# Retention values in one 512-wide pass with four resident weight slots, and sample state updates with zero-padded full-row operands

## The chip, the cores and the metric

The kernel runs on one core of a Trainium2 chip. The time is device microseconds (us) from the launch's first to its last instruction on that core, and runs are compared by their median. Five engines work in parallel, each through its own instruction queue in order: TensorE (PE, matmuls; PEld is its weight load), VectorE (DVE), ScalarE (ACT), GpSimd (POOL) and SyncE (SP, which here only issues DMAs). SBUF is the on-chip memory, PSUM the memory that matmuls write to.

## What is computed

One inference step of a two-layer decoder trunk for a prompt of 1024 tokens and a sample group of 8 sequences with 8 tokens each: layer 0 is sliding-window attention, layer 1 is retention in chunks of 128 tokens. The change touches layer 1 alone. Cut to it, the reference is:

```python
def retention_chunk(state, q, k, v, lg):          # one head: d = 256, e = 512
    a = jnp.einsum('bqhd,bshd->bhqs', q, k) * dmask[None]
    inner = jnp.einsum('bhqs,bshe->bqhe', a, v)
    cross = jnp.einsum('bqhd,bhde->bqhe', q, state) * decay
    new_state = jnp.exp(L * lg) * state + jnp.einsum('bshd,bshe->bhde', k_dec, v)
    return new_state, inner + cross

z = h @ w_in                  # (tokens, 1024) @ (1024, 6144): q 1024, k 1024, v 2048, gate 2048
q, k, v, g = jnp.split(z, [1024, 2048, 4096], axis=-1)
# prompt: 8 chunks of 128 tokens, state carried along; sample: one chunk of 8 tokens a sequence
y = (group_norm(o) * silu(g)) @ w_out
```

## The kernel before

All 1088 tokens (1024 of the prompt, 64 of the sample) go through each projection together. Each operand x of a projection is split into hi (rounded) and lo = x - hi, and a product is three matmuls: hi*hi, hi*lo, lo*hi. `split` does this with one ACT cast and one DVE subtraction (L281, L282).

**Weights.** They stream through in slots of 128x1024 numbers. `prep` takes the oldest raw slot (`wraw`, two buffers), splits it into `whi` and `wlo` (three buffers in `wpool`) and has SP load the next raw one; `slot` hands a ready pair to a projection. A pool named in `self.extra` for a slot number may hold that slot's split in place of `wpool`.

**Two forms of projection.** `pair_t` (and `quad_t`) keeps a weight slot stationary and streams 384 or 320 tokens (L135 to L137); it serves q, k, the gate and the output projections. `group_n` keeps 128 tokens stationary and streams weights, so that its result has tokens in rows; it serves the attention values (`first=True`) and, in layer 1, the retention values, 256 features at a time: two passes a head, each of two slots. A pass makes, for 8 token chunks and 8 slices of the inner dimension, three matmuls of 128x256 (L194 to L196), and for the sample chunk, whose stationary holds hi and lo side by side, two (L199, L200). Results go to the PSUM tile `pj` (two buffers, each of two halves of 512 columns), ACT scales them into `v1` (L871), POOL stores them to the DRAM scratch `s_v1` (L872).

**Layer 1.** `ret_qkv` for head 0 runs first. Then `weave` mixes, at `RATE_RET`, the projections of the rest (the gate of head h, then q, k, v of head h+1) with `ret_units`, a generator of 32 units, one for each head and chunk. A unit loads q, k and v back (`ret_load`), forms the masked scores (L944) and the transposed keys (L956), splits v (`split_v`), and in `ret_mid` makes the inner and cross products (L985 to L990) and the state update (L1002 to L1004), all of 128x512. The inner product of the first chunk is the first PE instruction of layer 1 that waits for v.

**Samples.** Beside the eight units of a head run eight steps of `ret_sample_step`. At the even ones the queries of four sequences, in `qpad`, multiply their stored states `s0`, each with 32 columns of the array (L1069, float32). At every step two sequences get their new state's increment: keys `ks` and values `vs` hold four sequences in 32 rows each (hi and lo twice), and one matmul takes the 32 rows of one sequence, `ks[r]` by `vs[r]` (L1080, PSUM tile `pa`, four buffers). DVE adds it to the scaled old state in place (L1083), POOL stores the new state (L1084). `ret_sample_load` has SP load four states for each even step (L1050, eight buffers) and, every fourth step, `ks` and `vs` (L1056, L1057).

**What sets the order.** The program text gives an order, but the tile framework's scheduler moves each instruction on each engine's queue by its own estimate of when its inputs are there. It puts single sample matmuls and pieces of a unit between the matmuls of a projection. Once built, each engine's order is fixed.

## Time and profile before

| | |
|---|---|
| median of 3 runs (lowest, highest) | 1697.99 us (1696.72, 1701.69) |
| the profiled execution | 1695.23 us |
| its span, first to last instruction | 1693.5 us, mean granted clock 0.999 |
| PE busy | 1668.0 us, 98% of the span |
| DVE, ACT, POOL busy | 988.7 (58%), 612.7 (36%), 340.0 (20%) us |
| DMA engines, mean traffic | 161 GB/s over the span |

A matmul's row gives its start and its latency; matmuls overlap, so what one costs the engine is the distance from its start to the next one's start, not its latency. Layer 1 up to the last unit lies between 655 and 1480 us of the span.

### The profile page before, as it was taken

To read this page: it belongs to the slowest core of one execution; us is meant where nothing else is said; L and a number is where in the kernel's file an instruction comes from. 1 tells how busy PE (TensorE), PEld (TensorE's weight loads), DVE (VectorE), ACT (ScalarE), POOL (GpSimd) and SP (SyncE) were. 2 spreads that over 40 slices of the span, in tenths; PEclk is the share of its full clock that TensorE was granted. 3 is DMA by queue.
4 is the path that set the end of the run, shared out by engine and by line. 5 is a ranking of instruction groups with operands and counts; after the bars stand their busy time and mean duration, and the time that the engine had idled before them with its cause. 6 is when DMAs were issued, how large, how long until landed. Compare 5 with 4: busy or idle time off the path is not lost.

```text
span 1693.5 us, 28264 instructions
## 1 busy us (share of the span) xinstructions
PE 1668.0 (98%) x10600; PEld 1583.5 (94%) x10600; DVE 988.7 (58%) x2184; ACT 612.7 (36%) x1365; POOL 340.0 (20%) x533
## 2 busy tenths in 40 slices
PE   8999999999999999999999999999999999999998
PEld 7989999988999999899999999999899988999998
DVE  7558787966248574246744655455744756443852
ACT  6245555777334341222222312322222432241421
POOL 1413312132001121211123212231122222200000
PEclk9999999999999999999999999999999999999999
DMA  8655646684315443254445544465454865482342
GB/s 288 174 142 154 168 118 170 178 273 166 119 36 173 144 146 119 80 165 154 155 165 183 184 154 160 151 188 177 146 163 146 279 199 172 167 256 86 122 143 87
DMA packets 178697, 273.15 MB, mean 161 GB/s; under 512 B 29968, under 2 KB 128336, under 8 KB 178528
## 3 DMA queue, kind: packets, MB, share of 16 engines
q1 hardware_dynamic: 141152, 177.94, 35.1%
q0 software_dynamic: 37408, 93.40, 15.7%
q8 instruction: 83, 1.36, 0.3%
q14 instruction: 54, 0.44, 0.1%
HBM read 173.45 MB, written 99.68 MB: 161 GB/s over the span
## 4 chain that ended last, share of the span: by engine, by line
PE 73%; issue 1%; DMA 0%; POOL 0%; ACT 0%; DVE 0%; POOLq 0%; ACTq 0%
PE pj L135 17%; PE pj L137 17%; PE pj L136 17%; PE pj L194 3%; PE pj L195 3%; PE pj L196 3%; PE pa L1080 1%; PE pa L1069 1%; PE pa L913 1%; PE pa L1002 1%; PE pa L1003 1%; PE pa L1004 1%; PE pa L944 1%; PE pa L987 1%; PE pa L986 1%
## 5 line engine op out<-in xcount | busy, mean ns | idle before, releaser
L135 PE MATMUL pj<-act,whi 128*128 128x384 f32 (+1 forms) x2160 | 711.9, 330 | 2.3 <-ACT ys L729 1.2
L137 PE MATMUL pj<-act,wlo 128*128 128x384 f32 (+1 forms) x2160 | 707.8, 328 | 0.0
L136 PE MATMUL pj<-act,whi 128*128 128x384 f32 (+1 forms) x2160 | 707.1, 327 | 0.0
L135 PEld LDWEIGHTS pj<-act,whi 128*128 128x128 f32 x2160 | 405.8, 188 | 11.7 <-issue 6.3
L137 PEld LDWEIGHTS pj<-act,wlo 128*128 128x128 f32 x2160 | 405.6, 188 | 4.2 <-issue 3.2
L136 PEld LDWEIGHTS pj<-act,whi 128*128 128x128 f32 x2160 | 405.8, 188 | 3.6 <-issue 2.0
L281 ACT CAST whi<-wraw 128x512 fp32r<-128x512 f32 (+1 forms) x226 | 127.9, 613 | 191.5 <-PE pj L136 150.6
L282 DVE TENSOR_TENSOR wlo<-wraw,whi 128x512 fp32r<-128x512 f32 (+1 forms) x226 | 146.7, 681 | 70.7 <-ACT whi L281 70.3
L194 PE MATMUL pj<-whi,act 128*128 128x256 f32 x528 | 149.0, 286 | 1.1 <-ACT v L871 0.6
L195 PE MATMUL pj<-wlo,act 128*128 128x256 f32 x528 | 148.7, 283 | 0.0
L196 PE MATMUL pj<-whi,act 128*128 128x256 f32 x528 | 147.9, 283 | 0.0
L194 PEld LDWEIGHTS pj<-whi,act 128*128 128x128 f32 x528 | 100.1, 191 | 7.2 <-issue 3.2
L195 PEld LDWEIGHTS pj<-wlo,act 128*128 128x128 f32 x528 | 101.0, 191 | 0.8 <-issue 0.2
L196 PEld LDWEIGHTS pj<-whi,act 128*128 128x128 f32 x528 | 100.6, 191 | 0.3 <-issue 0.2
L518 ACT ACTIVATE s_sb<-s_sb,nm 128x257 f32<-128x257 f32 (+2 forms) x136 | 65.7, 488 | 33.2 <-DVE nm L515 32.6
L871 ACT ACTIVATE v<-pj,rcol 128x256 f32<-128x256 f32 x64 | 29.9, 474 | 127.7 <-PE pj L196 91.7
L330 DVE TENSOR_TENSOR rp_a<-pj,cs 128x768 f32<-128x768 f32 (+1 forms) x39 | 35.6, 912 | 63.5 <-PE pj L137 63.5
L872 POOL DMA_DIRECT2D s_v<-v x64 | 35.4, 554 | 167.8 <-ACT v L871 167.6
L340 DVE TENSOR_TENSOR rp_b<-pj,rbc 128x768 f32<-128x768 f32 (+1 forms) x36 | 32.8, 910 | 50.8 <-PE pj L137 50.7
L959 ACT ACTIVATE kh<-pa,rdec 128x256 fp32r<-128x256 f32 (+1 forms) x36 | 17.0, 473 | 114.0 <-PE pa L956 113.4
L1083 DVE SCALAR_TENSOR_TENSOR s<-s,pa 128x512 f32<-128x512 f32 x64 | 42.2, 684 | 24.5 <-PE pa L1080 24.0
L342 ACT ACTIVATE rp_a<-rp_b 128x768 f32<-128x768 f32 (+1 forms) x36 | 29.2, 810 | 73.1 <-DVE rp_b L340 73.1
(233 smaller groups left out, 2556.6 us busy)
## 6 DMA issues: line engine op xcount, KB each, us to landing
wraw<-wt SPq DMA_DIRECT2D x110, 512.0 KB, 4.4
s<-st SPq DMA_DIRECT2D x64, 256.0 KB, 3.1
srs<-s POOLq DMA_DIRECT2D x64, 256.0 KB, 2.7
act<-s_og SPq DMA_DIRECT2D x48, 192.0 KB, 3.8
qst<-s_q SPq DMA_DIRECT2D x32, 256.0 KB, 4.5
qk<-s_qk SPq DMA_DIRECT2D x32, 256.0 KB, 3.5
s_v<-v POOLq DMA_DIRECT2D x64, 128.0 KB, 2.5
vv<-s_v SPq DMA_DIRECT2D x32, 256.0 KB, 2.7
```

The source lines that it names most:

```text
L135: mm(ps, hi[:, sl], a[c][:, 0], start=start and i == 0, stop=False)
L136: mm(ps, hi[:, sl], a[c][:, 1], start=False, stop=False)
L137: mm(ps, lo[:, sl], a[c][:, 0], start=False, stop=stop and i == last)
L194: mm(o, hi, w[0][:, sl], start=start, stop=False)
L195: mm(o, hi, w[1][:, sl], start=False, stop=False)
L196: mm(o, lo, w[0][:, sl], start=False, stop=stop)
L281: self.nc.scalar.copy(hi, x)
L282: self.nc.vector.tensor_tensor(out=lo, in0=x, in1=hi.bitcast(F32), op=ALU.subtract)
L330: nc.vector.tensor_tensor(out=ta, in0=ps, in1=self.cs[:, 0:1, c0:c0 + n].broadcast_to([P, 2, n]), op=ALU.mult)
L518: nc.scalar.activation(s[:, h, :], s[:, h, :], AF.Exp, bias=nm[:, h, :], scale=0.125, accum_out=den[:, h:h + 1])
L872: nc.gpsimd.dma_start(self.s_v1[h, i, :, g * 256:g * 256 + 256], st)
L1083: nc.vector.scalar_tensor_tensor(out=s0, in0=s0, scalar=float(gam ** 8), in1=pds[j], op0=ALU.mult, op1=ALU.add)
```

## The change

The retention values get their own routine, `group_v`: 512 features at a time in one pass a head, with four slots taken at once, so that one matmul streams 512 columns; a slot now holds two slices of 512 columns in place of four of 256. `group_n` keeps the attention values alone. The four splits are made earlier: `pair_t` for the keys calls `prep` also after the first half of its first two token blocks (`more`), and of the four slots of v the middle two are held in layer 1's own pool (`self.extra`); `wpool` keeps its three buffers. Results are evicted at 512 columns into the tile `rp_a`, and `v1` goes away.

In the sample update `kpad` holds, for each of four sequences, a full 128-row operand that is zero outside that sequence's 32 rows; SP writes the 32 rows of each by a DMA of its own. One matmul takes all 128 rows of `kpad[:, j]` by all of `vs`. All four sequences are updated at the even step, none at the odd one. The state tiles `s0` have four buffers, not eight. Loaded values go straight into the tile of their lo half, and `split_v` subtracts in place.

```diff
-    def pair_t(self, acts, evac, single=False):
+    def pair_t(self, acts, evac, single=False, more=False):
...
-                if c == 2:
+                if c == 2 or more and j == 0:
                     self.prep()
...
+    def group_v(self, acts, samp, evac):
+        ws = [self.slot() for _ in range(4)]
+        mm = self.nc.tensor.matmul
+        for i in range(9):
+            if i % 2 == 0:
+                ps = self.pj.tile([P, 2, 512], F32, name="pj")
+            o = ps[:, i % 2]
+            for kt in range(KT):
+                w = ws[kt // 2]
+                sl = slice(kt % 2 * 512, kt % 2 * 512 + 512)
+                first, last = kt == 0, kt == KT - 1
+                if i < 8:
+                    c, o0 = i // 3, i % 3 * P
+                    hi = acts[kt][c][:, 0, o0:o0 + P]
+                    lo = acts[kt][c][:, 1, o0:o0 + P]
+                    mm(o, hi, w[0][:, sl], start=first, stop=False)
+                    mm(o, hi, w[1][:, sl], start=False, stop=False)
+                    mm(o, lo, w[0][:, sl], start=False, stop=last)
+                else:
+                    both = samp()[:, kt, :]
+                    mm(o, both, w[0][:, sl], start=first, stop=False)
+                    mm(o, both, w[1][:, sl], start=False, stop=last)
+                    if kt in (1, 7):
+                        self.prep()
+                if kt % 4 == 3:
+                    if last:
+                        evac(i, o)
+                    yield 2.6
...
+        self.kpad = pool.tile([P, 4, P], F32R, name="kpad", bufs=1)
+        nc.gpsimd.memset(self.kpad.bitcast(F32), 0.0)
...
-            yield from self.pair_t(acts, evac)
-        for g in range(2):
-            def evac_v(i, ps):
-                st = pool.tile([P, 256], F32, name="v1", bufs=4)
...
-            yield from self.group_n(acts, lambda: self.samp, evac_v)
+            yield from self.pair_t(acts, evac, more=which)
+
+        def evac_v(i, ps):
+            st = pool.tile([P, 2, 384], F32, name="rp_a", bufs=3).rearrange("p a b -> p (a b)")[:, :512]
...
+        yield from self.group_v(acts, lambda: self.samp, evac_v)
...
-        v = pool.tile([P, 512], F32, name="vv1", bufs=2)[:n]
-        nc.sync.dma_start(v, self.s_v1[h, i, 0:n])
+        v = pool.tile([P, 512], F32R, name="vl1", bufs=3)[:n]
+        nc.sync.dma_start(v.bitcast(F32), self.s_v1[h, i, 0:n])
...
-            s0 = pool.tile([P, 512], F32, name="s0", bufs=8)
+            s0 = pool.tile([P, 512], F32, name="s0", bufs=4)
             nc.sync.dma_start(s0, self.io["st0"][4 * g + j, h, k * P:(k + 1) * P, :])
             u["s0"].append(s0)
+        b = 4 * g
+        for j in range(4):
+            nc.sync.dma_start(self.kpad[32 * j:32 * j + 32, j].bitcast(F32),
+                              self.s_kk[h, b + j, :, :, k * P:(k + 1) * P].rearrange("j l c -> (j l) c"))
...
-        if i % 2 == 0:
-            for j in range(4):
-                mm(po[32 * j:32 * j + 32], self.qpad[:, k, g, j], u["s0"][j], start=i == 0, stop=i == 6)
+        if i % 2:
+            return
+        for j in range(4):
+            mm(po[32 * j:32 * j + 32], self.qpad[:, k, g, j], u["s0"][j], start=i == 0, stop=i == 6)
...
-        pair = range(i % 2 * 2, i % 2 * 2 + 2)
-        pds = {}
-        for j in pair:
-            pds[j] = self.pa.tile([P, 512], F32, name="pa")
-            r = slice(32 * j, 32 * j + 32)
-            mm(pds[j], u["ks"][r, k * P:(k + 1) * P], u["vs"][r], start=True, stop=True)
-        for j in pair:
+        for j in range(4):
+            pd = self.pa.tile([P, 512], F32, name="pa")
+            mm(pd, self.kpad[:, j], u["vs"], start=True, stop=True)
...
+            self.extra = {L1_SLOT + 12 * h + i: pool for h in range(4) for i in (5, 6)}
...
+    def v_slots(w):
+        return list(w.reshape(4, 2, P, 512).transpose(0, 2, 1, 3).reshape(4, P, 1024))
```

Lines move by some twenty: L1069 of before is L1095 after, L1080 is L1103, L988 is L1011, L194 to L196 of the retention values are L236 to L238, L135 to L137 are L136 to L138. Counted over the whole of PE's queue, the scheduler's order holds the 64 query products L1069 in 19 unbroken runs before and L1095 in 27 after; the 64 updates L1080 stand in 48 runs before (32 alone, 16 of two). PE goes over between a matmul on the full array and one on a part of it 178 times before and 116 times after. Up to the first value matmul and from the second output projection to the end the two queues are the same but for line numbers.

Place A is on PE in head 0, where the first unit's inner product is fitted into the value matmuls. Before (in the names `act` is the stationary, `whi` and `wlo` stream; `vh` is the loaded value's hi half):

```order
L195 MATMUL pj<-wlo,act_6972 128x256
L196 MATMUL pj<-whi,act_6972 128x256
L988 MATMUL pa<-vh_8212,amh 128x512
L1002 MATMUL pa<-vh_8212,kh_8208 128x512 x2
L1069 MATMUL pa<-s_8306,qpad 32x512
```

After:

```order
L237 MATMUL pj<-wlo,act_6972 128x512
L238 MATMUL pj<-whi,act_6972 128x512
L979 MATMUL pa<-ident,qk_7947 128x128 x2
L1046 MATMUL pa<-qk_7999 64x64 x2
L979 MATMUL pa<-ident,qk_7999 64x128 x2
L1011 MATMUL pa<-vh_7971,amh 128x512
L1012 MATMUL pa<-vl_7949,amh 128x512
```

In both orders 48 value matmuls stand between the last one of the first chunk's values and this inner product; they are of 256 columns before and of 512 after, and the query products no longer follow it at once.

Place B is on PE in the last head, with the output projection (L135 to L137) around the sample steps. Before:

```order
L1080 MATMUL pa<-vst_15257,kh_15256 128x512
L137 MATMUL pj<-act_14774,wlo 128x320
L135 MATMUL pj<-act_14776,whi 128x320
L136 MATMUL pj<-act_14776,whi 128x320
L137 MATMUL pj<-act_14776,wlo 128x320
L1069 MATMUL pa<-s_15507,qpad 32x512
L1069 MATMUL pa<-s_15509,qpad 32x512
L1069 MATMUL pa<-s_15511,qpad 32x512
L1069 MATMUL pa<-s_15513,qpad 32x512
L135 MATMUL pj<-act_14762,whi 128x320
```

After:

```order
L1095 MATMUL pa<-s_14546,qpad 32x512
L138 MATMUL pj<-act_13534,wlo 128x384
L1095 MATMUL pa<-s_14548,qpad 32x512
L136 MATMUL pj<-act_13536,whi 128x384
L137 MATMUL pj<-act_13536,whi 128x384
L138 MATMUL pj<-act_13536,wlo 128x384
L136 MATMUL pj<-act_13538,whi 128x384
L137 MATMUL pj<-act_13538,whi 128x384
L138 MATMUL pj<-act_13538,wlo 128x384
L1095 MATMUL pa<-s_14550,qpad 32x512
```

The four query products of a step stood together and now stand singly; the updates L1103 come later and singly too, as full-array matmuls.

Place C is on SP in the last head, where DMAs for the next step are issued. Before (`s` is a state tile, `st` the stored states in DRAM, `wraw` a raw weight slot):

```order
L926 DMA vv_15400<-s_v_89 128x512
L107 DMA wraw<-wt 128x1024 x2
L1050 DMA s_15507<-st 128x512
L1050 DMA s_15509<-st 128x512
L924 DMA qk_15260<-s_qk_88 128x4x128
```

After:

```order
L1078 DMA kpad<-s_kk 32x128 [waits DMAHW6_49,PE_49]
L108 DMA wraw<-wt 128x1024 [waits DMAHW7_49,DVE_49]
L1078 DMA kpad<-s_kk 32x128 [waits PE_49]
L108 DMA wraw<-wt 128x1024 [waits DMAHW1_49,DVE_49]
L1074 DMA s_14287<-st 128x512 [waits DMAHW2_49,DMASW3_49]
```

The loads of `kpad`, each waiting for PE's use of the same rows in the step before, now stand ahead of weight loads and state loads in SP's queue.

## Rows read from the trace of the kernel before

**Rows 1.** Windows, after head 0's values: length, PE, PEld, DVE, ACT, POOL busy, clock.

```profile
725.00:1480.00 755.00, 755.00 (x4738) 694.39 (x4738) 418.36 (x803) 201.62 (x408) 176.52 (x272) 1.00 0.53 173
```

**Rows 2.** Timeline of PE, 256-wide values, then 512-wide unit matmuls: start, latency.

```profile
899.74 0.28 PE L196 MATMUL pj<-whi,act 128*128 128x256 f32 x1
...
902.14 0.28 PE L196 MATMUL pj<-whi,act 128*128 128x256 f32 x1
902.26 0.40 PE L988 MATMUL pa<-vh,amh 128*128 128x512 f32 x1
...
904.34 0.28 PE L199 MATMUL pj<-whi,samp 128*128 128x256 f32 x1
```

**Rows 3.** Timeline of PE: a run of 15 matmuls of 128x512 and what follows.

```profile
762.50 0.39 PE L985 MATMUL pa<-Sh,qh 128*128 128x512 f32 x1
...
765.91 0.33 PE L135 MATMUL pj<-act,whi 128*128 128x384 f32 x1
```

**Rows 4.** Timeline of PE: a single 32-row update among projection matmuls.

```profile
973.01 0.34 PE L136 MATMUL pj<-act,whi 128*128 128x384 f32 x1
973.28 0.49 PE L1080 MATMUL pa<-vst,kh 32*128 32x512 f32 x1
973.70 0.44 PE L137 MATMUL pj<-act,wlo 128*128 128x384 f32 x1
973.97 0.34 PE L135 MATMUL pj<-act,whi 128*128 128x384 f32 x1
974.15 0.34 PE L136 MATMUL pj<-act,whi 128*128 128x384 f32 x1
```

**Rows 5.** Timeline of PE: two updates of different rows in succession.

```profile
1021.64 0.50 PE L1080 MATMUL pa<-vst,kh 32*128 32x512 f32 x2
1022.07 0.41 PE L135 MATMUL pj<-act,whi 128*128 128x320 f32 x1
```

**Rows 6.** Timeline of PE: query products, two records each: a run of four, of two.

```profile
795.49 1.06 PE L1069 MATMUL pa<-s,qpad 128*32 128x512 f32 x8
796.48 0.50 PE L1080 MATMUL pa<-vst,kh 32*128 32x512 f32 x2
...
1376.12 1.05 PE L1069 MATMUL pa<-s,qpad 128*32 128x512 f32 x4
1377.10 0.44 PE L956 MATMUL pa<-ident,qk 128*128 128x128 f32 x2
```

**Rows 7.** Timeline of PE: the first two value matmuls after float32 transposes.

```profile
1068.45 0.36 PE L194 MATMUL pj<-whi,act 128*128 128x256 f32 x1
1068.65 0.28 PE L195 MATMUL pj<-wlo,act 128*128 128x256 f32 x1
```

**Rows 8.** Timeline of PE in head 0's values, with idle time before and its releaser.

```profile
691.36 0.39 PE L194 MATMUL pj<-whi,act 128*128 128x256 f32 x1 [0.61 <-ACT v L871]
...
702.19 0.79 PE L988 MATMUL pa<-vh,amh 128*128 128x512 f32 x1 [1.94 <-ACT vh L281]
...
724.03 0.44 PE L135 MATMUL pj<-act,whi 128*128 128x384 f32 x1 [0.56 <-ACT v L871]
```

**Rows 9.** Windows: the 3.6 us after the longest of these waits.

```profile
702.10:705.70 3.60, 3.51 (x12) 1.11 (x12) 0.69 (x1) 0.78 (x3) 1.07 (x2) 0.53 0.19 75
```

**Rows 10.** Chain that ended last, around that wait: start, us, what.

```profile
695.35 3.48 DMA s_v<-v
...
698.85 2.65 DMA vv<-s_v
```

**Rows 11.** Groups by line, DVE, 655 to 1480 us: busy, mean ns, idle before.

```profile
L1083 DVE SCALAR_TENSOR_TENSOR s<-s,pa 128x512 f32<-128x512 f32 x64 | 42.2, 684 | 24.5 <-PE pa L1080 24.0
```

**Rows 12.** DMA issues, 655 to 1480 us: count, size, median us to landing.

```profile
srs<-s POOLq DMA_DIRECT2D x64, 256.0 KB, 2.7
s<-st SPq DMA_DIRECT2D x56, 256.0 KB, 3.1
```

**Rows 13.** Waits of SP's own queue, 655 to 1480 us: total, times, longest.

```profile
SPq L1050 <- DMA srs<-s: 173.7, 47, 17.3
```

More of the change, by code (lines that the diff above doesn't have):

```diff
@@ L179, in sample_cols, with group_n @@
         return samp
-    def group_n(self, acts, samp, evac, first=False):
+    def group_n(self, acts, samp, evac):
         ws = self.slot(), self.slot()
@@ L200, in product @@
                 mm(o, both, w[1][:, sl], start=False, stop=stop)
-        if first:
-            last = self.pj.tile([P, 2, 512], F32, name="pj")
-            banks = [self.pa.tile([P, 512], F32, name="pa") for _ in range(3)] + [last[:, 0], last[:, 1]]
-            outs = [banks[i // 2][:, i % 2 * 256:i % 2 * 256 + 256] for i in range(9)]
-            for kt in range(KT):
-                for i in range(3):
-                    product(i, outs[i], kt, kt == 0 and i % 2 == 0, kt == KT - 1 and i % 2 == 1)
-            for i in range(3):
-                yield 2.6
@@ L211, in group_n @@
-        for i in range(3 if first else 0, 9):
-            if first:
-                o = outs[i]
-            else:
-                if i % 2 == 0:
-                    ps = self.pj.tile([P, 2, 512], F32, name="pj")
-                o = ps[:, i % 2, 0:256]
-            for kt in range(KT):
-                product(i, o, kt, kt == 0 and not (first and i % 2), kt == KT - 1 and (not first or i % 2 == 1 or i == 8))
+        last = self.pj.tile([P, 2, 512], F32, name="pj")
+        banks = [self.pa.tile([P, 512], F32, name="pa") for _ in range(3)] + [last[:, 0], last[:, 1]]
@@ L220, in group_n @@
+        outs = [banks[i // 2][:, i % 2 * 256:i % 2 * 256 + 256] for i in range(9)]
+        for kt in range(KT):
+            for i in range(3):
+                product(i, outs[i], kt, kt == 0 and i % 2 == 0, kt == KT - 1 and i % 2 == 1)
+        for i in range(3):
+            yield 2.6
+        for i in range(3, 9):
+            for kt in range(KT):
+                product(i, outs[i], kt, kt == 0 and i % 2 == 0, kt == KT - 1 and (i % 2 == 1 or i == 8))
                 if i == 8 and kt % 4 == 3:
@@ L221, in group_n @@
                     self.prep()
-            if not first:
-                evac(i, o)
             yield 2.6
-            if first:
-                for j in {5: range(3), 8: range(3, 9)}.get(i, ()):
-                    evac(j, outs[j])
+            for j in {5: range(3), 8: range(3, 9)}.get(i, ()):
+                evac(j, outs[j])
+    def group_v(self, acts, samp, evac):
[5 more added lines that the diff above has]
+            o = ps[:, i % 2]
+            for kt in range(KT):
+                w = ws[kt // 2]
[17 more added lines that the diff above has]
+                        evac(i, o)
+                    yield 2.6
@@ L479, in attn_v @@
         self.samp = None
-        yield from self.group_n(acts, samp, evac, True)
+        yield from self.group_n(acts, samp, evac)
     def attn_q(self, pool, acts, kv):
@@ L935, in split_v @@
         vh = pool.tile([P, 512], F32R, name="vh1", bufs=2)[:n]
-        vl = pool.tile([P, 512], F32R, name="vl1", bufs=2)[:n]
-        self.split(vh, vl, v)
-        return vh, vl
+        self.split(vh, v, v.bitcast(F32))
+        return vh, v
     def inner_a(self, pool, qk, n, mask):
@@ L1233, in weight_slots @@
     slots += t_slots(inp["w_ple_gate"][0])
+    assert len(slots) == L1_SLOT
     for h in range(4):
```

29 lines of the change are left out of this document (12 added, 17 removed).

## The prediction

> **What bounds the kernel now.** I read four views. The busy times by stretch come first: from 725 to 1480 us, where the units of layer 1 run beside the projections, PE is busy for all 755.00 us at the full clock of 2.4 GHz, DVE for 418 and ACT for 202 [rows 1]. Nobody else sets the end there; a microsecond less of PE work is a microsecond less of span, and a faster DVE or DMA is worth nothing. Second, PE's timeline, for what a matmul costs: its start to the next start. Third, the few places where PE is idle in layer 1: all lie in head 0's values, before 725 us [rows 8]. Fourth, the DMA rows, for what a wait could become.
>
> **Part 1, the values.** A 256-wide value matmul takes 0.120 us: 20 intervals between 899.74 and 902.14 [rows 2]. Fifteen unit matmuls of 512 columns take 3.41 us, 0.2273 us each [rows 3]. So 512 columns cost 1.89 times 256, not twice, since about 13 ns of each matmul do not grow with its columns. A pass has 8 chunks x 8 slices x 3 + 8 x 2 = 208 matmuls. Before: 4 heads x 2 passes x 208 = 1664 x 0.120 = 199.7 us. After: 832 x 0.2273 = 189.1 us. That is **-10.6 us**. The dearest 512-wide run that I found took 2.08 us for nine, 0.2311 us each [rows 2]; with it the gain is 7.4 us. I take the first, as its fifteen matmuls stand in an unbroken stream with projection matmuls on both sides, as the new ones will. The Trainium skill speaks against this term: "TensorE: Matmul & The Clock Gate", section "Back-to-back issue gap", gives N/2.4 + 2.5 ns for the gap at full clock, so only 2.5 ns a matmul could be saved, an estimated 2.1 us over 832 pairs in place of 10.6. The rows do not agree with it: 0.120 us is 13 ns over 256/2.4.
>
> Evictions are halved in number and doubled in width, on ACT; weight splits are as many as before. Splitting four slots needs 4 casts and 4 subtractions during the keys' matmuls, and in such a stretch ACT is idle for three quarters of the time and DVE for nearly half [rows 1], so I cost the moved preparation at nothing; if the cover failed, PE would stand at the fourth slot, needed only after 18 value matmuls (4 us) of a pass.
>
> **Part 2, the state updates.** A single 32-row update holds PE for 0.42 us (973.28 to 973.70). The full matmul before it takes 0.27 us to reach it, and the one after it 0.27 us, where 973.97 to 974.15 shows 0.17 to 0.18 undisturbed [rows 4]. So going over to a part of the array costs about 0.10 us, and going back as much. Two updates on different rows together take 0.43 us, no more than one [rows 5]. From PE's order:
> - updates: 48 runs x 0.425 = 20.4 us go; 64 full-array ones x 0.2273 = 14.5 us come: **-5.9 us**;
> - changes between full and part array: 178 to 116, 62 x 0.098 = **-6.1 us**;
> - query products: a run of four takes 0.99 us and a run of two 0.98 [rows 6], so a run costs the same however few are in it. 19 runs become 27: 8 x 0.99 = **+7.9 us**. This comes from the scheduler's placing [place B], not from the padding;
> - in PE's order 14 more blocks of transposes are followed by a full matmul, which costs 0.20 us in place of 0.12 [rows 7]: **+1.2 us**.
>
> Part 2 by itself is thus -2.9 us.
>
> **Part 3, head 0's start.** PE waits 1.94 us for the first chunk's value to come back from DRAM, and 0.61 and 0.56 us for evictions [rows 8]; one shorter wait of this kind is left out. After the long one the granted clock is 0.53 for 3.6 us [rows 9], that is mostly 1.2 GHz: at full clock this work would have taken about 1.9 us, so the wait cost another 1.7. The chain behind it is eviction, store (3.48 us), load (2.65) and cast [rows 10]; measured on PE it is 48 x 0.12 + 1.94 = 7.7 us from the chunk's last value matmul. After the change 48 matmuls of 512 columns stand there, 10.9 us [place A]: the chain has ended 3 us earlier, even if wider eviction and store add some tenths. The 1.94 and the 1.7 go. The 0.61 was paid between two passes; there is one pass now, so it goes. The 0.56 before the gate stays, and the wider eviction can add at most one 512-wide pass of DVE's size, 0.68 [rows 11]; I add 0.2. **-4.1 us**, with 0 and -4.8 as bounds.
>
> **Part 4, new waits.** States now have four buffers. A state's load must follow the update of the step before (DVE 0.68 [rows 11]), the store (2.7) and itself takes 3.1 [rows 12], with issue about 7 us. Adding up PE's new order at the prices above, from an update to the query product that needs the same buffer, the shortest distance is 11 us in three steps (one in head 2, two in head 3) and over 20 us in the rest. SP's queue is in order, and the loads of `kpad` in it wait for PE, with weight loads behind them [place C]; but SP stood 47 times for the state stores already, up to 17.3 us [rows 13], and PE waited for none of it [rows 1]. The bounds are 0, as in rows 1, and 8 us, a wait as in rows 8 with its clock loss (3.6) in two steps and some tenths elsewhere. I take **+2 us**, one wait of the size in rows 8.
>
> **The sum.** -10.6 - 5.9 - 6.1 + 7.9 + 1.2 - 4.1 + 2 = -15.6 us. The profiled execution took 1695.23 us, its span 1693.5 and 1.7 around it, which the change leaves alone; so a profiled run after should take 1679.6. The median of the runs stands 2.8 us higher at 1697.99, and less 15.6 gives **1682 us**. What is late next is PE again.
>
> **Rivals.**
> 1. *New waits eat most of it.* The three short state turnovers and the keys' four preparations each make PE wait 2 us and lose clock as in rows 9: 8 to 14 us come back, 1690 to 1696, say 1693. For it: in rows 8 the scheduler placed a matmul 1.9 us before its DRAM round trip was over, and the new turnovers are round trips. Against: 11 us of distance for 7 of chain.
> 2. *The padding loses what row groups gave.* If a lone 32-row update cost no more than a full one, 48 runs x 0.2273 = 10.9 us would become 14.5, +3.6 in place of -5.9, and the changes between array forms would cost nothing (+6.1 lost): with the other terms 1697.99 + 3.6 + 7.9 + 1.2 - 10.6 - 4.1 + 2 = 1698. Rows 5 speak for it, where two run at the price of one; rows 4 against it, where one alone holds PE for 0.42. The same page of the Trainium skill, section "Packing small matmuls — row/col tiling", has this rule: matmuls on different groups of 32 rows run concurrently, and one alone takes as long as a full one. The trace agrees with its first half and not with its second.
> 3. *The fixed part of a matmul shrinks.* The new stream costs 0.2311 or a little more, as in rows 2, and head 0's wait stays: 15.6 - 3.2 - 4.1 = 8.3 us of gain, 1690.
> 4. *Slower.* States come too late through SP. Each step's query products stand behind loads that stand behind the stores of the step before, and weights behind these. To lose 0.3% on top of the 17.6 us of gain without waits takes 23 us, that is 12 of the 16 steps with a wait of 1.9 us each. It decides from a chain of 13 us in the short turnovers and over 20 in the others, against 7 measured; price 1705. Only the 17.3 us of rows 13 speaks for it, and that is waiting for work that had not been done yet.
>
> **How the numbers follow.** Forecast 0.74 (1677 to 1688), rival 1 0.13, rival 2 0.04, rival 3 0.05, rival 4 0.04. The range runs from 1676 (no new waits, all of head 0's gain, and a median as near to the profiled run as 1 us) to 1692 (rival 3 and half of rival 1). About 0.3%, 5 us, is what a measurement here can tell from no change: faster by more is below 1692.9, with the forecast, rival 3 and half of rival 1, 0.85; the same 0.11; slower 0.04.
>
> **What would show it.** In the new profile 512-wide value matmuls start 0.227 to 0.231 us apart; full-array updates cost the same, with no 0.27 beside them; query products stand in about 27 runs of 0.99. PE waits in head 0 once, before the gate, and the clock does not fall. If PE's waits name state loads, `kpad` or `wraw`, part 4 was wrong; if the 512-wide stream runs at 0.24, part 1.

## The result, and the profile after

The changed kernel took 1687.97 us, the median of 4 runs (1685.8 to 1689.56), beside 1698.94 (1696.72 to 1701.69) for the kernel before: a ratio of 0.9934, 95% interval 0.9914 to 0.9954. Six more runs of it gave 1685.01 beside 1699.62, ratio 0.9919 (0.9902 to 0.9936). The prediction was 1682 with a range of 1676 to 1692; it is faster by 11 to 15 us, where 15.6 were forecast.

The page of the kernel after begins like this (span; busy time, share and instructions of each engine):

```profile
span 1684.0 us, 26627 instructions
...
PE 1658.8 (99%) x9768; PEld 1546.6 (92%) x9768; DVE 986.7 (59%) x2176; ACT 603.2 (36%) x1329; POOL 323.9 (19%) x498
```

The answer to [rows 1] is the window behind head 0's values (length; PE, PEld, DVE, ACT, POOL busy; clock; DMA share; GB/s):

```profile
725.00:1470.00 745.00, 745.00 (x4102) 663.70 (x4101) 415.75 (x794) 194.17 (x379) 162.11 (x244) 1.00 0.54 176
```

PE is still busy for every microsecond of it, at the same clock. Of all PE's waits from 640 to 1530 us there is one left (engine, tile and line, releaser: total, times, longest):

```profile
PE pj L136 <- ACT rp_a L894: 0.8, 1, 0.8
```

That is the wait before head 0's gate, 0.56 us in [rows 8], now longer by the wider eviction (0.69 us in place of 0.47, mean of the ACT groups). The 1.94 and the 0.61 of [rows 8] are gone, and no state load, `kpad` or weight has become a wait.

Two rows of PE's timeline answer to [rows 2]: 21 intervals of a value stream, 512 columns wide (start, latency, what).

```profile
702.13 0.40 PE L237 MATMUL pj<-wlo,act 128*128 128x512 f32 x1
...
707.02 0.40 PE L237 MATMUL pj<-wlo,act 128*128 128x512 f32 x1
```

4.89 us for 21, 0.2329 each. Over the whole trace the mean of 691 neighbouring starts in value streams is 0.2319 us, with most at 0.226, 0.231, 0.233 or 0.236. In the kernel before 1469 such neighbours, 256 wide, stood 0.1197 apart.

Where the time went is seen best between two landmarks, the same two projection matmuls counted from the first: one 2 us ahead of head 0's first value matmul, one some 20 us behind the last unit of layer 1. In the kernel before, first profile, then in the kernel after:

```profile
661.50 0.31 PE L136 MATMUL pj<-act,whi 128*128 128x320 f32 x1
...
1498.69 0.33 PE L137 MATMUL pj<-act,wlo 128*128 128x384 f32 x1
```

```profile
665.29 0.31 PE L137 MATMUL pj<-act,whi 128*128 128x320 f32 x1
...
1488.11 0.33 PE L138 MATMUL pj<-act,wlo 128*128 128x384 f32 x1
```

They lie 837.19 us apart before and 822.82 after. Call this distance the stretch (the expectations quoted below call it layer 1, and its first landmark where layer 1 begins). The change gains 14.4 us in it, 3.8 us are lost ahead of it and 1.1 behind. The experiments below read the stretch, since it repeats better than any time of a whole run.

### The profile page after: what moved, and what is told of

Read it like the earlier page. It is cut to its first block, busy times and chain, and to the rows that moved or that the text cites. A ratio compares the mean times of both kernels' runs of the same rounds, so it can differ in the third digit from the quotient of the medians.

```text
span 1684.0 us, 26627 instructions
## 1 busy us (share of the span) xinstructions
PE 1658.8 (99%) x9768; PEld 1546.6 (92%) x9768; DVE 986.7 (59%) x2176; ACT 603.2 (36%) x1329; POOL 323.9 (19%) x498
## 4 chain that ended last, share of the span: by engine, by line
PE 72%; DVE 1%; DMA 1%; issue 0%; ACT 0%; POOLq 0%; ACTq 0%
PE pj L136 16%; PE pj L138 16%; PE pj L137 16%; PE pj L236 4%; PE pj L237 4%; PE pj L238 4%; PE pa L1095 2%; PE pa L1103 1%; PE pa L1025 1%; PE pa L1027 1%; PE pa L1026 1%; PE pa L967 1%; PE pa L936 1%; PE pa L1008 1%; PE pa L1009 1%; PE pa L1010 1%
## 5 line engine op out<-in xcount | busy, mean ns | idle before, releaser
L136 PE MATMUL pj<-act,whi 128*128 128x384 f32 (+1 forms) x2160 | 711.3, 329 | 2.3 <-ACT ys L750 1.0
L138 PE MATMUL pj<-act,wlo 128*128 128x384 f32 (+1 forms) x2160 | 708.0, 328 | 0.0
L137 PE MATMUL pj<-act,whi 128*128 128x384 f32 (+1 forms) x2160 | 707.7, 328 | 0.0
L136 PEld LDWEIGHTS pj<-act,whi 128*128 128x128 f32 x2160 | 406.5, 188 | 11.0 <-issue 3.7
L137 PEld LDWEIGHTS pj<-act,whi 128*128 128x128 f32 x2160 | 406.4, 188 | 3.4 <-issue 0.8
L138 PEld LDWEIGHTS pj<-act,wlo 128*128 128x128 f32 x2160 | 406.2, 188 | 3.5 <-issue 1.7
L236 PE MATMUL pj<-whi,act 128*128 128x512 f32 x256 | 102.6, 401 | 0.0
L237 PE MATMUL pj<-wlo,act 128*128 128x512 f32 x256 | 101.0, 395 | 0.0
L238 PE MATMUL pj<-whi,act 128*128 128x512 f32 x256 | 100.5, 394 | 0.0
L894 ACT ACTIVATE rp_a<-pj,rcol 128x512 f32<-128x512 f32 x32 | 22.0, 688 | 126.4 <-PE pj L238 94.8
L236 PEld LDWEIGHTS pj<-whi,act 128*128 128x128 f32 x256 | 48.1, 188 | 17.0 <-issue 3.4
L238 PEld LDWEIGHTS pj<-whi,act 128*128 128x128 f32 x256 | 48.0, 188 | 11.1
L237 PEld LDWEIGHTS pj<-wlo,act 128*128 128x128 f32 x256 | 48.1, 188 | 10.2
L926 POOL TENSOR_TENSOR br<-bv,mhalf 128x1 f32<-128x1 f32 x36 | 29.8, 829 | 127.6 <-DVE bv L923 127.6
L823 DVE SCALAR_TENSOR_TENSOR ple_st<-ple_st,pleh 128x768 f32<-128x768 f32 (+2 forms) x25 | 22.0, 880 | 51.8 <-ACT ple_st L822 51.8
L1106 POOL DMA_DIRECT2D srs<-s x64 | 35.7, 559 | 85.7 <-DVE s L1105 84.8
```

What stands on the lines that cost most here:

```text
L136: mm(ps, hi[:, sl], a[c][:, 0], start=start and i == 0, stop=False)
L137: mm(ps, hi[:, sl], a[c][:, 1], start=False, stop=False)
L138: mm(ps, lo[:, sl], a[c][:, 0], start=False, stop=stop and i == last)
L236: mm(o, hi, w[0][:, sl], start=first, stop=False)
L237: mm(o, hi, w[1][:, sl], start=False, stop=False)
L238: mm(o, lo, w[0][:, sl], start=False, stop=last)
```

## Experiments

### Both kernels once more: what belongs to the change

Neither kernel is edited here; both are profiled a second time.

> The changed kernel once more, unaltered, for a second profile and a narrower ratio. Theory: layer 1 gains 14 us and nothing before it belongs to the change, since the engines' queues up to layer 1 are the same in both kernels; the 5.7 us for which PE stood for the scores' first softmax piece (with the clock at 0.86 around it), and the 0.85 us in the finish, are then the run's, not the kernel's: the wait comes back at another length (before: 2.9 us), and layer 1 again begins to end in 822.8 us, against 837.1 before. Median 1686 to 1690. Rival: the change causes the loss ahead of layer 1 (another program in memory, other addresses); then the wait is again over 5 us and layer 1 again begins 3 to 5 us later than in the kernel before. Times of the median can't tell these apart by themselves, the profile can.

> The kernel before once more, unaltered, for a second profile. Where layer 1 begins has come out at 661 (before), 665 and 666 (the changed kernel, twice), 669, 670 and 666 us (three relatives of it), while the two profiles of the changed kernel agree on layer 1 itself to 0.02 us. Theory: ahead of layer 1 the time differs from run to run, with the kernel the same; here layer 1 begins anywhere from 660 to 670, and lasts 837.2 us as in the first profile of the kernel before. Rival, the change costs 4 us ahead of layer 1: layer 1 begins again within 1 us of 661.

Measured: the changed kernel's stretch is 822.82 us again, to the hundredth. Its first landmark stands at 666.17 us; in the second profile of the kernel before, at 666.40 in place of 661.50. So the rival falls: ahead of the stretch the time differs from run to run. In the eleven further profiles of this study and the two first ones the landmark lay between 661.5 and 673.0 us. Up to 6.7 us of that arise by 145 us, where attention starts, the rest in attention behind it. PE's waits from 95 to 130 us, in the first and then in the second profile of the kernel before:

```profile
PE pa L605 <- ACT s_sb L575: 2.2, 1, 2.2
PE pa L567 <- DMA wraw<-wt: 0.7, 1, 0.7
```

```profile
PE pa L605 <- ACT s_sb L575: 3.8, 1, 3.8
PE pa L567 <- DMA wraw<-wt: 2.7, 1, 2.7
```

and in the two profiles of the changed kernel, first and second:

```profile
PE pa L626 <- ACT s_sb L596: 5.1, 1, 5.1
```

```profile
PE pa L626 <- ACT s_sb L596: 5.8, 1, 5.8
```

The wait for the first softmax piece and the waits for loads (`wraw`) come to 2.9 to 6.5 us, differently each time, with the same queues. The 1.1 us behind the stretch are not the change's either: its second profile spends 194.8 us there, like the kernel before, its first 195.9.

The part on the stretch fell: the kernel before took 835.30 us in its second profile, not 837.2.

```profile
666.40 0.31 PE L136 MATMUL pj<-act,whi 128*128 128x320 f32 x1
...
1501.70 0.33 PE L137 MATMUL pj<-act,wlo 128*128 128x384 f32 x1
```

The reason stands in head 0. PE's waits from 640 to 1530 us in this profile are

```profile
PE pa L988 <- ACT vh L281: 1.6, 1, 1.6
PE pj L194 <- ACT v L871: 0.6, 1, 0.6
PE pj L135 <- ACT v L871: 0.6, 1, 0.6
PE pj L199 <- ACT v L871: 0.3, 1, 0.3
```

The long one is 1.60 us (1.94 in [rows 8]), and the 3.6 us behind it look like this, to be held against [rows 9]:

```profile
706.70:710.30 3.60, 3.55 (x25) 2.31 (x26) 0.69 (x1) 0.73 (x2) 1.07 (x2) 1.00 0.19 75
```

The clock is 1.00, and PE starts 25 matmuls in the time in which it started 12 before. With the state updates of the change alone (below) the wait was 2.02 us, and with eight buffers 1.88; both times the clock stayed at 1.00 as well. So the 1.7 us of lost clock were one run's, not the kernel's, and 835.3 is the fairer base: against it the change gains 12.5 us in the stretch.

### The padding: undone, with and without its order

First, the changed kernel with the state updates as they were (`ret_sample_load`, `ret_sample_step` and the loaded values; the core of it):

```diff
-        for j in range(4):
-            pd = self.pa.tile([P, 512], F32, name="pa")
-            mm(pd, self.kpad[:, j], u["vs"], start=True, stop=True)
+        pair = range(i % 2 * 2, i % 2 * 2 + 2)
...
+        for j in pair:
+            pds[j] = self.pa.tile([P, 512], F32, name="pa")
+            r = slice(32 * j, 32 * j + 32)
+            mm(pds[j], u["ks"][r, k * P:(k + 1) * P], u["vs"][r], start=True, stop=True)
```

> The changed kernel with the old state updates (32-row matmuls in pairs, over eight steps, values loaded into the tile that is split, five state buffers since eight do not fit beside the wide values). In PE's order: 27 runs of query products as in the changed kernel, 53 runs of 32-row updates in place of 64 full-array ones, 208 changes between full and part of the array against 116. Theory (prices from the rows of before, full-array matmul at 0.232 us): against the changed kernel 53 x 0.425 - 64 x 0.232 = +7.7, 92 x 0.098 = +9.0, the fourteen dearer transposes gone -1.2: +15.5 us, so 1703. Rival, that padding gives nothing (a lone 32-row update costs a full one's time and the changes between forms nothing): 53 x 0.23 - 14.8 = -2.6 and -1.2, so 1684. A rival on the four buffers: if waits for states cost anything in either kernel, PE's waits name state loads.

Second, nothing but the padding undone, four updates in one step as in the change (the keys come packed, by one DMA, in place of the four into `kpad`):

```diff
             pd = self.pa.tile([P, 512], F32, name="pa")
-            mm(pd, self.kpad[:, j], u["vs"], start=True, stop=True)
+            r = slice(32 * j, 32 * j + 32)
+            mm(pd, u["ks"][r, k * P:(k + 1) * P], u["vs"][r], start=True, stop=True)
```

> The changed kernel with nothing but the padding undone: the four state updates still stand in one step of two, but each is a 32-row matmul on its own row group of the packed keys in place of a full-row one on zero-padded keys. In PE's order 55 runs of 32-row updates in place of 64 full-array ones, 212 changes between full and part of the array in place of 116, query products in 26 runs in place of 27. Theory: 55 x 0.425 - 64 x 0.232 = +8.5, 96 x 0.098 = +9.4, less 1.0 for the run of query products and 1.2 for the transposes: layer 1 is 15.7 us longer than in the changed kernel, about 1701. Rival, a lone 32-row matmul costs what a full one does and the changes nothing: 64 x 0 - 9 x 0.23 - 1.2, 3 us shorter. Rival in between, only the changes cost or only the 32 rows do: 8 to 9 us longer.

Measured: the first took 1700.20 us, ratio to the kernel before 1.0003 (0.9990 to 1.0017), its stretch 839.29 us, **16.5 us** more than in the changed kernel (15.5 expected). The second took 1700.90, ratio 1.0007 (0.9993 to 1.0022), its stretch 839.83, **17.0 us** more (15.7 expected). The rival that padding gives nothing wanted both shorter than the changed kernel, and falls.

The price is seen in the timelines. The same place in the program, first with 32-row updates (the second of the two kernels), then with the padded ones (the changed kernel):

```profile
991.85 0.42 PE L136 MATMUL pj<-act,whi 128*128 128x320 f32 x1
992.10 0.31 PE L137 MATMUL pj<-act,whi 128*128 128x320 f32 x1
992.34 0.49 PE L1101 MATMUL pa<-vst,kh 32*128 32x512 f32 x1
992.76 0.41 PE L138 MATMUL pj<-act,wlo 128*128 128x320 f32 x1
993.01 0.31 PE L136 MATMUL pj<-act,whi 128*128 128x320 f32 x1
```

```profile
990.61 0.30 PE L136 MATMUL pj<-act,whi 128*128 128x320 f32 x1
990.75 0.31 PE L137 MATMUL pj<-act,whi 128*128 128x320 f32 x1
990.90 0.40 PE L1103 MATMUL pa<-vst,kpad 128*128 128x512 f32 x1
991.13 0.31 PE L138 MATMUL pj<-act,wlo 128*128 128x320 f32 x1
991.28 0.32 PE L136 MATMUL pj<-act,whi 128*128 128x320 f32 x1
```

With 32 rows the projection matmul ahead takes 0.24 to hand over, the update 0.42, the one behind 0.25; padded they take 0.15, 0.23 and 0.15. One lone update thus costs 0.91 - 0.53 = 0.38 us more. The two halves of [rows 4]'s reading, the update itself and a change on either side, are both there.

That the wide values alone give no gain at all is the order's doing: the query products stand in 27 runs in place of 19, the 32-row updates in 53 in place of 48, and there are 208 changes in place of 178. At the prices above that is 8 x 0.99 + 5 x 0.425 + 30 x 0.098 = 13.0 us more, while the values and the waits of head 0 give some 8.6 back; against the second profile of the kernel before the stretch is 4.0 us longer.

### State updates alone, with four buffers and with eight

The kernel before with `kpad`, one step in two, and `s0` with four buffers as in the change; then the same with

```diff
-            s0 = pool.tile([P, 512], F32, name="s0", bufs=4)
+            s0 = pool.tile([P, 512], F32, name="s0", bufs=8)
```

> The kernel before with the state updates of the change alone (zero-padded full-row operands, one step in two, four state buffers, values split in place); the values stay 256 wide in two passes. In PE's order: 26 runs of query products against 19, 114 changes between full and part array against 178. Theory: 7 x 0.99 = +6.9, 64 x 0.232 - 48 x 0.425 = -5.6, 64 x 0.098 = -6.3, transposes +1.2: -3.8 us against the kernel before, so 1695, and head 0's 1.94 us wait with the clock falling behind it is still there. Rival, padding gives nothing: +6.9 + 64 x 0.232 - 48 x 0.232 + 0 + 1.2 = +11.8, so 1711. Rival, four buffers make PE wait: PE's waits name state loads, 1697 or more.

> The kernel before with the state updates of the change alone, and eight state buffers as before in place of four. In PE's order the query products stand in 21 runs in place of 26 with four buffers, and there are 104 changes in place of 114. Theory, the four buffers cost through the order alone, by breaking the query products apart: 5 x 0.99 + 10 x 0.098 = 5.9 us less in layer 1 than with four buffers, 10.4 us less than in the kernel before, so 1689. Rival, four buffers cost through waits for the states: the difference stands in PE's waits, and is 0.9 us, the one wait for a state load that the profile with four buffers has. Rival, what the order costs goes with the products and not with their runs: no difference beyond the changes, 1 us.

Measured: with four buffers 1696.42 us, ratio 0.9986 (0.9972 to 1.0000), stretch 832.67 us: 4.5 less than in the first profile of the kernel before and 2.6 less than in the second. Theory had -3.8; with the 2.02 us that head 0 waits here (1.60 in the second profile) and one wait of 0.9 us it is -2.5, as measured. With eight: 1690.97 us, ratio 0.9956 (0.9935 to 0.9977), stretch 824.96 us, **7.7 us** less than with four, where 5.9 were expected. PE's waits from 725 to 1490 us with four buffers:

```profile
PE pa L1074 <- DMA s<-st: 0.9, 1, 0.9
PE pj L135 <- ACT v L873: 0.6, 1, 0.6
```

and with eight:

```profile
PE pj L135 <- ACT v L873: 0.6, 1, 0.6
```

So waiting for states explains 0.9 of the 7.7. The order, with its 26 runs of query products against 21, carries most of the rest: added up over PE's rows between the landmarks, each matmul charged up to the next start, the query products take 26.3 us with four buffers and 20.8 with eight. Four state buffers are expensive although PE stands idle for them only once.

### Four states in one tile

The same cause, taken away where memory has no room for more buffers: one load for the four states of a step, so that their products become ready together.

```diff
-        u["s0"] = []
-        for j in range(4):
-            s0 = pool.tile([P, 512], F32, name="s0", bufs=4)
-            nc.sync.dma_start(s0, self.io["st0"][4 * g + j, h, k * P:(k + 1) * P, :])
-            u["s0"].append(s0)
+        s0 = pool.tile([P, 4, 512], F32, name="s0", bufs=1)
+        nc.sync.dma_start(s0, self.io["st0"][4 * g:4 * g + 4, h, k * P:(k + 1) * P, :].rearrange("j p e -> p j e"))
+        u["s0"] = [s0[:, j] for j in range(4)]
```

> The changed kernel with the four states of a step in one tile, fetched by one DMA (one buffer), in place of four tiles and four DMAs, so that a step's four query products become ready together. In PE's order they stand in 21 runs in place of 27 and there are 104 changes between full and part array in place of 116. Theory (a run of query products costs 0.99 us however few are in it, and a change 0.098): 6 x 0.99 + 12 x 0.098 = 7.1 us less, 1681, if the single state tile brings no waits. Rival: what the four products cost is theirs and not their run's, then 1688. Rival: with one buffer the next load stands until the last of four stores has read the tile, and PE waits for it; up to 16 steps x 1 us, so 1690 to 1697.

Measured: 1678.47 us, ratio 0.9871 (0.9852 to 0.9891); the stretch is 815.72 us, **7.10** less than in the changed kernel, where 7.1 were worked out. A step late in layer 1 shows it. In the changed kernel its four products stand in four runs of one (two records are one product, as in [rows 6]), of which the first and the third are:

```profile
1387.94 1.04 PE L1095 MATMUL pa<-s,qpad 128*32 128x512 f32 x2
1388.92 0.44 PE L136 MATMUL pj<-act,whi 128*128 128x384 f32 x1
...
1395.87 1.04 PE L1095 MATMUL pa<-s,qpad 128*32 128x512 f32 x2
1396.84 0.45 PE L138 MATMUL pj<-act,wlo 128*128 128x384 f32 x1
```

and with one tile in two runs of two:

```profile
1394.19 1.05 PE L1093 MATMUL pa<-s,qpad 128*32 128x512 f32 x4
1395.17 0.66 PE L936 MATMUL pa<-ident,on 128*128 128x128 f32 x4
...
1396.20 1.05 PE L1093 MATMUL pa<-s,qpad 128*32 128x512 f32 x4
1397.18 0.45 PE L138 MATMUL pj<-act,wlo 128*128 128x384 f32 x1
```

A run of one product holds PE for 0.97 to 0.98 us, to the start of the next matmul, and one of two for as long. The one buffer brings no waits: from 725 to 1520 us PE has none.

### Is it the width?

The values in one pass on four resident slots, as in the change, but with each 512-wide matmul issued as two of 256:

```diff
-                    mm(o, hi, w[0][:, sl], start=first, stop=False)
-                    mm(o, hi, w[1][:, sl], start=False, stop=False)
-                    mm(o, lo, w[0][:, sl], start=False, stop=last)
+                    for e in range(2):
+                        h0 = slice(kt % 2 * 512 + e * 256, kt % 2 * 512 + e * 256 + 256)
+                        oe = o[:, e * 256:e * 256 + 256]
+                        mm(oe, hi, w[0][:, h0], start=first and e == 0, stop=False)
+                        mm(oe, hi, w[1][:, h0], start=False, stop=False)
+                        mm(oe, lo, w[0][:, h0], start=False, stop=last and e == 1)
```

> The changed kernel with its values still in one pass on four resident slots, but each 512-wide matmul issued as two 256-wide ones into halves of the same tile: 1664 matmuls in place of 832. Everything else of the change stays; in PE's order the query products stand in 22 runs in place of 27, with 106 changes in place of 116, which is worth 5 x 0.99 + 10 x 0.098 = 5.9 us less. Read in layer 1, which repeats to a few hundredths. Theory, 512 columns cost 0.232 in a long stream: 1664 x 0.120 - 832 x 0.232 = +6.7, less 5.9, layer 1 is 0.8 us longer than in the changed kernel. Rival, 0.2273 as the prediction took it: +10.6 less 5.9, 4.7 us longer. Rival, a matmul's columns alone count, and the gain of the change came from one pass in place of two: 5.9 us shorter. The Trainium skill, "TensorE: Matmul & The Clock Gate", section "Back-to-back issue gap", with its 2.5 ns a matmul would give an estimated +2.1 less 5.9, 3.8 us shorter.

Measured: 1682.54 us, ratio 0.9903 (0.9882 to 0.9925); the stretch is 817.59 us, **5.2 us shorter** than in the changed kernel. My theory, 0.8 longer, missed by 6; of the rivals, the one by which columns alone count comes nearest, with 5.9 shorter. The timeline says why: 256-wide matmuls are not all alike. Twelve in this kernel, and eight a little later in the same pass:

```profile
678.09 0.28 PE L241 MATMUL pj<-whi,act 128*128 128x256 f32 x1
...
679.34 0.27 PE L240 MATMUL pj<-wlo,act 128*128 128x256 f32 x1
```

```profile
700.08 0.28 PE L241 MATMUL pj<-whi,act 128*128 128x256 f32 x1
...
700.92 0.28 PE L239 MATMUL pj<-whi,act 128*128 128x256 f32 x1
```

1.25 us for 11 intervals is 0.1136, 0.84 for 7 is 0.120. Of 1479 neighbouring starts 40% lie at most 0.115 us apart and the mean is 0.1168; in the kernel before it is 0.5% and 0.1197. With 0.1168 the sum is 1664 x 0.1168 - 832 x 0.2319 = +1.4, less 5.9. The 0.8 us for which the changed kernel waits before head 0's gate are gone here too (PE has no wait in this stretch), which makes it -5.3 for -5.2 measured. So the width itself, as far as this pair shows it, is worth about 1.4 us. The other 4.8 us of the values' gain lie between 256-wide matmuls here and in the kernel before, and so in something else that the change moved. Two candidates: the halves of the output by turns, or where the weight slots lie.

The halves one after the other, the rest the same:

```diff
-                    for e in range(2):
-                        h0 = slice(kt % 2 * 512 + e * 256, kt % 2 * 512 + e * 256 + 256)
+            for e in range(2):
+                oe = o[:, e * 256:e * 256 + 256]
+                for kt in range(KT):
+                    w = ws[kt // 2]
+                    h0 = slice(kt % 2 * 512 + e * 256, kt % 2 * 512 + e * 256 + 256)
```

> The kernel with 256-wide matmuls on four resident slots once more, but a slice's two halves one after the other: 24 matmuls in a row into the first half of the tile, then 24 into the second, as the kernel before does it, in place of three and three by turns. In PE's order nothing else differs (22 runs, 106 changes). The runs of 256-wide matmuls started 0.117 us apart with the halves by turns, and 0.120 in the kernel before. Theory, what made them cheaper is the change of output and of the stationary slice every three matmuls: here 0.120 again, layer 1 is 1664 x 0.0032 = 5.3 us longer than with the halves by turns. Rival, it is which weight slots lie where: 0.117 here too, layer 1 the same within 1 us.

Measured, in one run: stretch 817.42 us against 817.59, mean spacing 0.1166 with 42% at most 0.115. Apart from the halves' order only one update and four projection matmuls stand elsewhere on PE. The alternation does nothing.

Then the slots alone. The kernel with the state updates of the change and the old values (two passes, four buffers), with two of each head's value slots in layer 1's pool (two other tiles give up buffers for them):

```diff
         with tc.tile_pool(name="l1", bufs=2) as pool:
+            self.extra = {40 + 12 * h + i: pool for h in range(4) for i in (5, 6)}
             self.ret_const(pool)
```

> The kernel with the state updates of the change alone, 256-wide values in two passes, once more, and of each head's four value slots the second and third put into layer 1's own pool, where the change puts them; two tiles elsewhere have two buffers in place of four and three to make room (evictions may wait for that, only the spacing of the matmuls is read). In PE's order nothing differs. Two of a head's eight-slice halves' slots are thus where they were with 256-wide matmuls on four resident slots, where 40% of the starts lay 0.113 to 0.115 us apart and the mean was 0.1168; in the kernel before 0.5% lay so and the mean was 0.1197. Theory, it is where the slots lie in SBUF: here 20 to 40% at 0.113 to 0.115 and a mean of 0.117 to 0.1185. Rival, it is that four slots are resident and the pass is one: 1% and 0.1197, as with the slots where they were.

Measured, in one run: a mean of 0.1170 and 36% at most 0.115 (1448 neighbours), against 0.1197 and 1% with the slots where they were. PE's order is not the same throughout, though the expectation says so: runs and changes of form are as many, but behind the first 238 value matmuls of head 0 instructions stand in other places. Up to there the order is the same, and the spacing differs as much: 0.1172 with 36% against 0.1198 with 0.4%. Of the first 24 of them the first twelve stream from a slot that stayed and the last twelve from a moved one (the 1st, 7th, 13th and 19th wait for the casts of the slots' halves). The 1st, 12th, 16th and 24th are:

```profile
665.24 0.28 PE L194 MATMUL pj<-whi,act 128*128 128x256 f32 x1
...
666.55 0.28 PE L196 MATMUL pj<-whi,act 128*128 128x256 f32 x1
...
667.03 0.28 PE L194 MATMUL pj<-whi,act 128*128 128x256 f32 x1
...
667.94 0.28 PE L196 MATMUL pj<-whi,act 128*128 128x256 f32 x1
```

1.31 us for 11 intervals is 0.119, 0.91 for 8 is 0.114; with the slots where they were the latter is 0.96, or 0.120. So where the slots lie, or what else of the pool's tiles moves with them, sets the spacing; one pass and four resident slots are not needed for it. What in the placement does it stays open.

Nor are the moved slots the better ones at any width. In the first 24 value matmuls of a head in the changed kernel, 512 wide, the twelve from the moved slots start 0.233 us apart, those ahead and behind 0.231 (mean of heads 0 to 2). Width and place thus do not simply add up: with 0.231 for all, the wide matmuls would gain an estimated 1664 x 0.1197 - 832 x 0.231 = 7.0 us if all slots had stayed, a kernel that no run shows.

The closer spacing did not make the stretch of this kernel shorter: it is 833.51 us, against 832.67 with the slots where they were. PE's waits come to 7.0 us in place of 4.4, three of them for states, and behind the longest, of 2.38 us, the granted clock is 0.53 for 3.6 us, mostly 1.2 GHz:

```profile
PE pa L1074 <- DMA s<-st: 3.2, 3, 2.4
```

```profile
855.90:859.50 3.60, 3.60 (x19) 3.60 (x19) 0.00 (x0) 0.00 (x0) 0.00 (x0) 0.53 0.68 252
```

### The two together

256-wide values by turns, with the one state tile, which the scheduler puts in the fewest runs yet:

> The 256-wide matmuls with halves by turns on four resident slots, and the four states of a step in one tile by one DMA. In PE's order 17 runs of query products and 96 changes, against 21 and 104 with 512-wide matmuls and one state tile (layer 1 815.7 us), and 22 and 106 with 256-wide ones and four state tiles (817.6 us). Theory, the price is the run's: 1664 x 0.117 - 832 x 0.232 = +1.7, less 4 x 0.99 and 8 x 0.098: layer 1 is 3.0 us shorter than the first, 812.7; from the second, 5 x 0.99 + 10 x 0.098 = 5.9 less, 811.7. Rival, waits for the one state tile: PE's waits name it, and layer 1 stays above 815.

Measured: 1674.25 us, ratio 0.9876 (0.9856 to 0.9896); the stretch 812.78 us, 2.9 less than with 512-wide values and one tile, where 3.0 were expected. PE's waits in it:

```profile
PE pa L1031 <- DVE sgl L1124: 0.6, 1, 0.6
PE pa L1099 <- DMA s<-st: 0.2, 1, 0.2
```

This and the one-tile kernel are the better versions. Both beat the kernel before and the changed one; their ratios, 0.9876 and 0.9871, do not tell them apart, but the shorter stretch says that the wide matmuls are not what one would keep the change for.

## Why the prediction was right, and where its steps were off

| kernel | query-product runs | changes of form | stretch, us | median, us |
|---|---|---|---|---|
| before, first and second profile | 19 | 178 | 837.19, 835.30 | 1698.9 |
| after, first and second profile | 27 | 116 | 822.82, 822.82 | 1688.0, 1685.0 |
| values alone | 27 | 208 | 839.29 | 1700.2 |
| padding undone | 26 | 212 | 839.83 | 1700.9 |
| state updates alone, 4 buffers | 26 | 114 | 832.67 | 1696.4 |
| state updates alone, 8 buffers | 21 | 104 | 824.96 | 1691.0 |
| after, one state tile | 21 | 104 | 815.72 | 1678.5 |
| after, 256 wide | 22 | 106 | 817.59 | 1682.5 |
| after, 256 wide, one state tile | 17 | 96 | 812.78 | 1674.3 |

**The bound** was right: in every one of these kernels PE is what ends last in layer 1, with waits of no more than 4.4 us in the stretch, and its work, counted from its order, gave the stretch where the price of its matmuls was known.

**Part 1** is the step with the wrong size. It took 0.2273 us for 512 columns from a short run of units [rows 3]; the long stream costs 0.2319, close to the dearer 0.2311 of [rows 2], which I had put down as the bound. 832 x 0.2319 = 192.9 against 1664 x 0.1197 = 199.2: -6.3 us in place of -10.6. Its explanation was wrong as well. It read a fixed part of 13 ns that two narrow matmuls pay twice; the same narrow matmuls go down to 0.1136 where the operands lie otherwise, 7 ns over 256/2.4. The Trainium skill's N/2.4 + 2.5 ns ("TensorE: Matmul & The Clock Gate", section "Back-to-back issue gap") lies below all of these rows. What it said of the width, some 2 us, is near the 1.4 that the 256-wide kernel showed; the 4.8 us that lie between 256-wide matmuls in the two places it doesn't have. The gain of -6.3 can't be split further between width and place, since they do not add up (above).

**Part 2** was right in each price. A lone update cost 0.42 and its changes 0.10 each side, the runs of query products 0.97 to 1.00 however few were in them (-7.10 for -7.1), and the part by itself, in one kernel, gave -2.6 us where -2.5 were worked out with the waits that it really had. With 0.2319 for the full-array updates the forecast's -2.9 becomes -2.6. Its remark that the 7.9 us come from the scheduler's placing holds: with eight buffers five of the seven runs that the state updates add are gone again. The second rival, that padding loses, wanted kernels without it 3 us faster; they are 16 to 17 slower.

**Part 3** was half right. The 1.94 and the 0.61 went, and the last wait grew by 0.2, as put down; the shorter wait that it left out, 0.3, went as well. The 1.7 us for the clock were counted as the kernel's, and belonged to the profiled run: in three other profiles with a wait of 1.6 to 2.0 us at that place the clock stayed at 1.00. Taken from the second profile the term is -1.60 - 0.61 - 0.3 + 0.2 = -2.3 rather than -4.1.

**Part 4** came out at 0 rather than +2: no wait names states, `kpad` or weights. The four buffers cost through the order, which Part 2 had, and not through waits. The first and the fourth rival fall with it. The third had half of it, the smaller gain per column, but head 0's wait did go.

Put together: -6.3 - 2.6 - 2.3 = -11.2 us, against -12.5 in the stretch. Added up over PE's rows between the landmarks, the second profile of the kernel before against the changed kernel, the query products come to +7.8 (worked out: +7.9), the values to -6.8 (-6.3), the updates to -5.0 (-5.6), the waits to -2.3 (-2.3), and all the rest, with the changes of form and the transposes, to -6.2 (-4.9). The 1.3 us that are missing thus lie in the rest and in the values, while the updates gave less; both runs without padding, too, were dearer by 1.0 and 1.3 than worked out. From 1698.9 the two give 1686 to 1688, and the medians are 1685 and 1688. The forecast of 1682 was low by what the values, the clock and the waits of head 0 were overcounted, 6.1 us, and the updates 0.3, less 2 for waits that did not come. That these errors have opposite signs is luck: without the 2 the forecast would have stood at 1680.

## What to carry to other kernels

Where one engine is busy throughout, count its order in runs and in changes of array form, price each from the trace, and the sum predicts a stretch to a microsecond or two, as it did here wherever the matmuls' prices came from the same placement; a buffer count can cost several microseconds through that order with no wait to be seen. Take the price of a matmul from a long stream of its own kind, and don't carry it to another place of memory: its width may not be what moves it. A single profile holds accidents (a clock that fell at a place in one profile of four, a start that differs by 10 us), so a second profile of the same kernel belongs to the pricing of a wait or a clock loss.

## What was unexpected of the hardware

Matmuls of one shape, on the same engine at clock 1.00 with nobody waiting, start mostly 0.113 or 0.120 us apart (256 columns), and 0.226, 0.231 or 0.233 to 0.236 (512 columns); placing two of four weight slots in another pool moved the mean at 256 columns from 0.1197 to 0.1170, while at 512 columns the matmuls of these slots stand wider apart than the others (0.233 against 0.231); what decides is open. A wait of 1.94 us was followed by a granted clock of 0.53 for 3.6 us, mostly the level of 1.2 GHz, in one profile, while waits of 1.60, 1.88 and 2.02 us at the same place left it at 1.00, 2.4 GHz; in the kernel with two slots moved alone, a wait of 2.38 us elsewhere was followed by 0.53 for 3.6 us too. And the way to the first landmark, with the same queues in all kernels, took anything within 11.5 us, while the stretch of the changed kernel repeated to the hundredth.
